# A hybrid decoder layer: feed-forward loads begun at the scores' end, token transposes further back, the bias table in other banks

## The chip, the cores and the metric

The kernel runs on one core of a Trainium2 chip. The metric is the device time of one execution in microseconds, lower is better. A core has a matrix engine (PE, its weight loads shown as PEld), a vector engine (DVE), an activation engine (ACT), a general engine (POOL) and a queue engine (SP). SP and POOL start the DMA transfers between HBM and on-chip memory; POOL can also start one that adds what it brings to what is there. Matrix products land in eight PSUM banks, which DVE and ACT read.

## The reference

One layer on a sequence of 512 tokens of 1024 values, float32. Three groups of attention heads share one input projection; their outputs are joined, projected by `w_out` (1024 x 1024) and added to `x`; a feed-forward of width 4096 and a last norm follow.

```python
h = rmsnorm(x, norm1_w)
proj = h @ w_in
aq, ak, av, bq, bk, bv, br, ba, cq, ck, cv = jnp.split(proj, ...)
y_a = dilated_attention(heads(aq, 6), heads(ak, 6), heads(av, 6), bias_a)
y_b = gla(heads(bq, 4), heads(bk, 4), heads(bv, 4), br, ba, w_a2, b_a, gla_norm_w)
y_c = moba_attention(heads(cq, 6), heads(ck, 6), heads(cv, 6), bias_c)
mix = jnp.concatenate([y_a, y_b, y_c], axis=-1)
x = x + mix @ w_out
h2 = rmsnorm(x, norm2_w)
x = x + jnp.square(jax.nn.relu(h2 @ w_ff1)) @ w_ff2
return rmsnorm(x, final_norm_w)
```

## The kernel before

**Arithmetic.** Each float32 operand of a large product is split into a high part, rounded to PE's fast format (ACT writes it, tiles `wh`, `xh`, `mh`, `yp`, `Ah`), and the rest (DVE subtracts, `wl`, `xl`, `ml`, `Al`); three products of halves (high by high, low by high, high by low) make up one. The large products are also cut into 2 x 2 blocks and done with seven block products instead of eight (`PRODUCTS`, numbered 0 to 6; the out-projection takes them in `O_ORDER` = 0, 1, 3, 5, 2, 4, 6). The weights of products 2 to 6 are sums of quarters of the matrix, formed either by loads on POOL that accumulate in the raw buffer `wraw` or by DVE. Every weight goes the same way: SP loads 512 KB into `wraw`, ACT and DVE split it (`parts`), PE uses it. `ip` 0 and 1 are the two halves of a product's inner dimension.

**Stages in time.** Projections and gated attention, to about 100 us (`qkps` are PE's products of queries and keys for the projections, `vt` the bias table); scores, softmax and values (`sps`, `ptp`, `po`), to about 200; the out-projection (`ops`), about 185 to 245, whose results DVE adds to `x` (tiles `x3`, shown as `x`); the root mean square of each token (`m`, `tmp`, `y`), the scaled tokens (`y0`, shown as `y`), their transposes on PE into a bank `yps`, and the copies out of it (`yf`), from which the feed-forward's token parts `yp` are made; then the feed-forward until 561: `f1X`, `f1Y` and `f1Z` are its first layer, `f2X` and so on its second.

**What sets the order.** The program is written as streams: generators that yield one instruction or a group of matmuls at a time. A planner (`Plan`) runs them once, before anything is built, keeps a clock for each engine from a cost for every instruction, and always issues the instruction that could begin first, with a stream's priority as the second key (lower first). A stream can `take` and `give` a resource (a PSUM bank of the pools "mm", "s", "pt", "o" and "g", a weight slot "w", a buffer "big", a raw slot "rawo"), `wait` for a key that another stream fires, or `spawn` a stream. What comes out is a fixed order on each engine; a change of one wait moves rows far from it, on every engine.

**The streams that the change touches.** `bias_table` makes the table of relative biases in two products on PE; `fetch_o` loads the out-projection's weights and `cut_o` splits them; `out_proj` issues its matmuls; `y_out` scales and transposes the tokens; `fetch_ff` loads the feed-forward's weights, `cut_ff` splits them, and `fewer` and `give("w")` pass weight slots between the two. The key "scores" is fired when the last scores are done, "turns" when the last attention output is turned, "o cut" when all of `w_out` is split. All instructions are recorded by one helper, so each carries line L129 in the profile; they are told apart by their tiles.

Of the kernel before, what the change touches and what calls it, by code (L numbers as in the profile page):

```python
# [100 lines left out]
class Plan:  # L101
# [14 lines left out]
    def spawn(self, gen, prio=0):  # L116
        self.streams.append(dict(gen=gen, prio=prio, item=None, at=self.now, sent=None, n=len(self.streams)))

    def fire(self, key, t=None):
        self.done[key] = self.now if t is None else t  # L120

    def give(self, res):
        self.free[res].append(self.now)
# [26 lines left out]
    def run(self):  # L150
        while self.streams:
            cand, moved = None, False
            for st in list(self.streams):
                while True:
                    if st["item"] is None:
                        try:
                            moved = True
                            self.now = st["sent"] if st["sent"] is not None else st["at"]
                            st["item"] = st["gen"].send(st["sent"])
                        except StopIteration:  # L160
                            self.streams.remove(st)
                            break
                    it = st["item"]
                    if isinstance(it, tuple):
                        kind, key = it
                        if kind == "prio":
                            st["prio"] = key
                        elif kind == "wait":
                            if key not in self.done:
                                break  # L170
                            st["at"] = max(st["at"], self.done[key])
                        else:
                            if not self.free[key]:
                                break
                            t = min(self.free[key])
                            self.free[key].remove(t)
                            st["at"] = max(st["at"], t)
                        st["sent"], st["item"] = st["at"], None
                        continue
                    o = self.best(st)  # L180
                    first = o[0] if isinstance(o, list) else o
                    t = max(self.start(x, st["at"]) for x in (o if isinstance(o, list) else [o]))
                    if cand is None or (t, st["prio"], st["n"]) < cand[:3]:
                        cand = (t, st["prio"], st["n"], st, o)
                    break
            if cand is None:
                if moved:
                    continue
                if self.streams:
                    raise RuntimeError("streams wait for ever")  # L190
                return
            t, _, _, st, o = cand
            end = 0.0
            for x in o if isinstance(o, list) else [o]:
                end = max(end, self.issue(x, t))
            st["item"], st["sent"] = None, end
# [3 lines left out]
def hybrid_block_kernel(ctx: ExitStack, tc: tile.TileContext, xT_d, x_d, w0_d, wv_d, wqk_d, wo_d, w1_d, w2_d,  # L200
# [10 lines left out]
    spawn, fire, give = plan.spawn, plan.fire, plan.give  # L211
    late = dict(copy=LC, tt=LT)

    def slot(name, dt=F32, shape=(128, 512)):
        return sp.tile(list(shape), dt, name=name, tag="slot", bufs=SLOTS)

    def big(name, dt=F32, shape=(128, 1024)):
        return wp.tile(list(shape), dt, name=name, tag="big", bufs=BIGS)
# [4 lines left out]
    def bank(tag, name):  # L223
        return ps.tile([128, 512], F32, name=name, tag=tag, bufs=BANKS[tag])
# [183 lines left out]
    def o_plus(n, ip, t, qs):  # L408
        for q in qs:
            yield POOL.dma_start(t, wo_d[q[0], q[1], ip], accum_op=OP.add)  # L410
        VB["o", n, ip] = t
        fire(("oB", n, ip))
# [8 lines left out]
                fire(("x3", t, half))  # L421

    def fetch_o():
        for n, q, more in ((0, (0, 0), None), (1, (1, 0), None), (5, (1, 1), None), (4, (0, 1), ((1, 1),)),
                           (6, (1, 0), ((0, 0), (0, 1), (1, 1)))):
            for ip in range(2):
                yield ("take", "rawo")
                yield ("take", "big")
                VB["o", n, ip] = t = big("wraw")
                yield SP.dma_start(t, wo_d[q[0], q[1], ip])  # L430
                if more:
                    spawn(o_plus(n, ip, t, more), 3)
                else:
                    fire(("oB", n, ip))

    def cut_o():
        for n in O_ORDER:
            for ip in range(2):
                yield ("wait", ("oB", n, ip))
                t = VB["o", n, ip]  # L440
                yield from parts(("o", n, ip), t)
                if n in (0, 3):
                    spawn(o_plus(2 if n else 3, ip, t, ((1 if n else 0, 1),)), 3)
                else:
                    give("rawo")
                    give("big")

        fire("o cut")

    XS = {}  # L450
    units = [(i, c) for c in range(NC) for i in (1, 2)]
# [22 lines left out]
    def give_raw():  # L474
        give("big")
        give("raw2")
# [81 lines left out]
            yield ("take", "w")  # L558

    def cut_ff():  # L560
        yield ("wait", "o cut")
        for u in units:
            for o, (n, *_) in enumerate(PRODUCTS):
                if u == units[0] or u == units[1]:
                    yield ("prio", 0.5 if u == units[0] else 3)
                if u == units[-1]:
                    if o == 0:
                        for _ in range(3):
                            give("w")
                    yield ("prio", 1.5 + o)  # L570
                for ip in range(2):
                    yield ("wait", ("B", u, n, ip))
                    yield from parts((u, n, ip), B[u, n, ip])
                    fire(("cut", u, n, ip))
                    if n in (1, 4, 6):
                        give_raw()
# [69 lines left out]
    def bias_table(oneh):  # L646
        yield ("wait", "R")
        for i in range(2):
            yield ("take", "mm")
            vt = bank("mm", "vt")  # L650
            yield PE.matmul(vt[:, :320], rb, oneh[i], start=True, stop=True)
            vals = slot("vals", shape=(12, 320))
            yield DVE.tensor_copy(vals, vt[:12, :320])
            give("mm")
            yield POOL.dma_start(tab[:, i * 320:(i + 1) * 320], vals)
        fire("tab")

# [2 lines left out]
    st = {}  # L660
# [577 lines left out]
    def y_out(t, half, y):  # L1238
        y0 = slot("y0")
        yield Any(DVE.tensor_scalar(y0, x3[t, half], y, None, op0=OP.mult), ACT.activation(y0, x3[t, half], AF.Copy, scale=y))  # L1240
        r = "og"[half] if t % 2 else "pt"
        yield ("take", r)
        pt = bank(r, "yps")
        yield [PE.transpose(pt[:, i * 128:(i + 1) * 128], y0[:, i * 128:(i + 1) * 128], ident) for i in range(4)]
        ts = slice(t % 2 * 128, t % 2 * 128 + 128)
        ks = range(half * 4, half * 4 + 4)
        src = [pt[:, i * 128:(i + 1) * 128] for i in range(4)]
        if t % 2 == 0:
            yf[half, t // 2] = [new("yf") for _ in range(2)]
        else:  # L1250
            yield ("wait", ("yf", t - 1, half))
        for i, k in enumerate(ks):
            out, scale = yf[half, t // 2][i // 2][:, i % 2, ts], nw2[:, k:k + 1]
            yield Any(ACT.activation(out, src[i], AF.Copy, scale=scale), DVE.tensor_scalar(out, src[i], scale, None, op0=OP.mult))
        give(r)
        fire(("yf", t, half))
# [50 lines left out]
    def out_proj():  # L1307
# [39 lines left out]
        for n in O_ORDER:  # L1347
            if n == 1:
                yield ("wait", "scores")
                for q in range(2):  # L1350
                    yield from part(n, q, (0, 1, 2))
                yield ("wait", "turns")
                for q in range(2):
                    yield from part(3, q, (0, 1, 2))
                spawn(fetch_ff(), 4)
                spawn(cut_ff(), 3)
                spawn(y_parts(), 0.4)
            for q in range(2):
                yield from part(n, q, (3,) if n in (1, 3) else (0, 1, 2, 3))
            give_w()  # L1360
            give_w()
            if n in (2, 3):
                give("big")
                give("big")
            if n == 2:
                give("w")
                give("w")
            give("raw2")

    hq = {}  # L1370
# [343 lines left out]
```

## Time and profile before

| | |
|---|---|
| median of three runs | 574.91 us (573.92 to 576.64) |
| profiled execution | 574.53 us, of which the span 572.8 |
| granted clock of PE over the span | 0.996 |
| PE busy | 555.9 us, 97% of the span, 3513 matmuls |
| DVE busy | 480.9 us, 84%, 879 instructions |
| ACT busy | 372.4 us, 65% |
| POOL busy | 71.1 us, 12% |
| moved by DMA | 99.73 MB, mean 174 GB/s |

The profile shows one execution. Its page gives the busy time of each engine, the chain of work that ended last, groups of instructions (output and inputs by tile name, count, mean duration, idle time before them and what ended it), and the DMA issues with the time to their landing. Beside it stand answers on the trace: waits by name, busy time by stretch, and timelines, each row with its start and duration, the instruction, and in brackets how long the engine had stood idle and what released it.

### The profile page before, as it was taken

What the parts mean: (1) busy time and instruction counts of PE and PEld (TensorE: products, weight loads), DVE (VectorE), ACT (ScalarE), POOL (GpSimd) and SP (SyncE); (2) the same over time, 40 slices, a digit from 0 to 9 for tenths busy, and PEclk for the clock granted to TensorE, in tenths of its full rate; (3) what the DMA queues carried; (4) which work ended last, traced back from release to release, by engine and by line L of the source; (5) the groups of instructions that cost most, each with busy time, mean ns of one, the idle gap of its engine ahead of it and who ended that gap; (6) DMA issues with size and microseconds to landing.
All of it is one profiled execution on the core that took longest, in us unless ns stands there. A gap on an engine that the chain in (4) does not pass through costs nothing.

```text
span 572.8 us, 9467 instructions
## 1 busy us (share of the span) xinstructions
PE 555.9 (97%) x3513; PEld 478.6 (84%) x3513; DVE 480.9 (84%) x879; ACT 372.4 (65%) x662; POOL 71.1 (12%) x93
## 2 busy tenths in 40 slices
PE   9999999999999999998999999999999999999994
PEld 8977887886786767788988899988999888999883
DVE  5899899977876988799799996799967799867993
ACT  6755644795865775788785466855467655579543
POOL 4012110001011011101212002020020110112101
PEclk9999999999999999999999999999999999999998
DMA  8944694396087549965988529787278594395812
GB/s 287 405 116 114 112 239 107 111 376 124 5 165 195 153 119 271 243 213 129 229 241 166 171 95 243 239 147 217 92 160 278 133 195 157 96 215 112 147 54 94
DMA packets 30813, 99.73 MB, mean 174 GB/s; under 512 B 3744, under 2 KB 3786, under 8 KB 30768
## 3 DMA queue, kind: packets, MB, share of 16 engines
q0 software_dynamic: 10032, 35.62, 34.4%
q1 hardware_dynamic: 20448, 63.25, 31.7%
q8 instruction: 27, 0.44, 0.3%
q10 hardware_dynamic: 288, 0.27, 0.1%
q14 instruction: 18, 0.15, 0.1%
HBM read 97.00 MB, written 2.13 MB: 173 GB/s over the span
## 4 chain that ended last, share of the span: by engine, by line
PE 85%; DVE 8%; ACT 3%; issue 1%; DMA 1%; SPq 0%; DVEq 0%; ACTq 0%
PE f2X L129 15%; PE f1X L129 15%; PE qkps L129 11%; PE f2Z L129 8%; PE f1Z L129 7%; PE vps L129 6%; PE ops L129 4%; PE f2Y L129 4%; PE f1Y L129 3%; PE sps L129 2%; PE po L129 2%; PE ptp L129 2%; DVE wl L129 2%; PE av L129 1%; DVE yf L129 1%; PE lp L129 1%
## 5 line engine op out<-in xcount | busy, mean ns | idle before, releaser
L129 DVE TENSOR_TENSOR wl<-wraw,wh 128x1024 fp32r<-128x1024 f32 (+2 forms) x174 | 191.3, 1109 | 36.0 <-ACT wh L129 35.8
L129 ACT ACTIVATE wh<-wraw 128x1024 fp32r<-128x1024 f32 (+2 forms) x173 | 164.3, 965 | 54.7 <-DVE x L129 9.7
L129 PE MATMUL f1X<-yp,wh 128*128 128x256 f32 x512 | 92.7, 283 | 0.0
L129 PEld LDWEIGHTS f1X<-yp,wh 128*128 128x128 f32 x512 | 80.1, 192 | 0.3
L129 POOL DMA_DIRECT2D wraw<-in_w x46 | 40.4, 952 | 273.8 <-DVE wl L129 205.2
L129 PE MATMUL f1X<-yp,wl 128*128 128x256 f32 x256 | 72.4, 283 | 0.0
L129 PE MATMUL f2X<-wh,Al 128*128 128x512 f32 (+1 forms) x132 | 50.5, 383 | 0.0
L129 PE MATMUL f2X<-wh,Ah 128*128 128x512 f32 (+1 forms) x132 | 50.5, 383 | 0.0
L129 PE MATMUL f2X<-wl,Ah 128*128 128x512 f32 (+1 forms) x132 | 50.5, 383 | 0.0
L129 PEld LDWEIGHTS f1X<-yp,wl 128*128 128x128 f32 x256 | 49.1, 192 | 0.0
L129 PE MATMUL f1Z<-yp,wh 128*128 128x256 f32 x256 | 46.3, 283 | 0.0
L129 PE MATMUL qkps<-xh,wh 128*128 128x512 f32 x96 | 40.8, 425 | 1.6 <-DVE vals L129 1.2
L129 ACT ACTIVATE h<-h 128x512 f32<-128x512 f32 x56 | 34.7, 625 | 11.5 <-DVE h L129 11.0
L129 PEld LDWEIGHTS f1Z<-yp,wh 128*128 128x128 f32 x256 | 39.9, 192 | 0.0
L129 ACT ACTIVATE Ah<-h 128x512 fp32r<-128x512 f32 x40 | 24.2, 620 | 22.2 <-DVE h L129 22.2
L129 PE MATMUL f1Z<-yp,wl 128*128 128x256 f32 x128 | 36.4, 284 | 1.8 <-DVE wl L129 1.8
L129 PE MATMUL qkps<-xh,wl 128*128 128x512 f32 x96 | 37.6, 392 | 0.0
L129 PE MATMUL qkps<-xl,wh 128*128 128x512 f32 x96 | 37.5, 391 | 0.0
L129 ACT ACTIVATE P<-P,mn 128x512 f32<-128x512 f32 (+3 forms) x48 | 26.5, 554 | 14.3 <-DVE mn L129 14.1
L129 PEld LDWEIGHTS f2X<-wl,Ah 128*128 128x128 f32 x132 | 24.8, 188 | 4.8
L129 PEld LDWEIGHTS f2X<-wh,Al 128*128 128x128 f32 x132 | 24.8, 188 | 4.8
L129 PEld LDWEIGHTS f2X<-wh,Ah 128*128 128x128 f32 x132 | 24.8, 188 | 4.7
(261 smaller groups left out, 1229.9 us busy)
## 6 DMA issues: line engine op xcount, KB each, us to landing
wraw<-in_w SPq DMA_DIRECT2D x66, 512.0 KB, 5.7
wraw<-in_w POOLq DMA_DIRECT2D x46, 512.0 KB, 6.4
wraw<-in_wqk SPq DMA_DIRECT2D x12, 512.0 KB, 6.5
wraw<-in_wo POOLq DMA_DIRECT2D x12, 512.0 KB, 7.4
wraw<-in_wv SPq DMA_DIRECT2D x10, 512.0 KB, 7.1
wraw<-in_wo SPq DMA_DIRECT2D x10, 512.0 KB, 6.2
wraw<-in_wv POOLq DMA_DIRECT2D x8, 512.0 KB, 5.8
nb<-tab SPq DMA_DIRECT2D x12, 256.0 KB, 4.8
```

Of the source, the lines that this page charges most:

```text
L129: getattr(getattr(self.nc, op.eng), op.method)(*op.args, **op.kw)
```

## The change

- The bias table's two products take a bank of the pool "s" (the scores' banks) instead of "mm".
- A new item of a stream, `("delay", t)`, puts its next instruction `t` us later on the planner's clock. It costs nothing on the chip. `y_out` yields 2.0 of it before the transposes.
- `fetch_ff` and `cut_ff` are spawned when the scores end, before product 1's first matmuls, instead of after product 3's first ones. `cut_ff` waits for product 4's split before it begins and for product 6's before the third of its products, instead of for all of `w_out`. The priority of product 6's split is 0.4. Two weight slots are given back after "turns" instead of after product 2.
- The weights of the out-projection's product 6 (the sum of all four quarters) are no longer loaded into their own buffer by a load on SP and three accumulating ones on POOL for each half. They are made from product 2's buffer (a sum of three quarters) by one accumulating load, after product 2 is split. On SP the loads of `w_out` go from 10 to 8, on POOL from 12 to 8.

```diff
--- before.py
+++ after.py
@@ -165,6 +165,8 @@
                         kind, key = it
                         if kind == "prio":
                             st["prio"] = key
+                        elif kind == "delay":
+                            st["at"] += key
                         elif kind == "wait":
                             if key not in self.done:
                                 break
@@ -421,8 +423,7 @@
                 fire(("x3", t, half))
 
     def fetch_o():
-        for n, q, more in ((0, (0, 0), None), (1, (1, 0), None), (5, (1, 1), None), (4, (0, 1), ((1, 1),)),
-                           (6, (1, 0), ((0, 0), (0, 1), (1, 1)))):
+        for n, q, more in ((0, (0, 0), None), (1, (1, 0), None), (5, (1, 1), None), (4, (0, 1), ((1, 1),))):
             for ip in range(2):
                 yield ("take", "rawo")
                 yield ("take", "big")
@@ -435,17 +436,19 @@
 
     def cut_o():
         for n in O_ORDER:
+            if n == 6:
+                yield ("prio", 0.4)
             for ip in range(2):
                 yield ("wait", ("oB", n, ip))
                 t = VB["o", n, ip]
                 yield from parts(("o", n, ip), t)
-                if n in (0, 3):
-                    spawn(o_plus(2 if n else 3, ip, t, ((1 if n else 0, 1),)), 3)
+                if n in (0, 3, 2):
+                    m, q = {0: (3, (0, 1)), 3: (2, (1, 1)), 2: (6, (1, 0))}[n]
+                    spawn(o_plus(m, ip, t, (q,)), 3)
                 else:
                     give("rawo")
                     give("big")
-
-        fire("o cut")
+            fire(("o cut", n))
 
     XS = {}
     units = [(i, c) for c in range(NC) for i in (1, 2)]
@@ -558,9 +561,10 @@
             yield ("take", "w")
 
     def cut_ff():
-        yield ("wait", "o cut")
         for u in units:
             for o, (n, *_) in enumerate(PRODUCTS):
+                if u == units[0] and o in (0, 2):
+                    yield ("wait", ("o cut", 6 if o else 4))
                 if u == units[0] or u == units[1]:
                     yield ("prio", 0.5 if u == units[0] else 3)
                 if u == units[-1]:
@@ -646,12 +650,12 @@
     def bias_table(oneh):
         yield ("wait", "R")
         for i in range(2):
-            yield ("take", "mm")
-            vt = bank("mm", "vt")
+            yield ("take", "s")
+            vt = bank("s", "vt")
             yield PE.matmul(vt[:, :320], rb, oneh[i], start=True, stop=True)
             vals = slot("vals", shape=(12, 320))
             yield DVE.tensor_copy(vals, vt[:12, :320])
-            give("mm")
+            give("s")
             yield POOL.dma_start(tab[:, i * 320:(i + 1) * 320], vals)
         fire("tab")
 
@@ -1238,6 +1242,7 @@
     def y_out(t, half, y):
         y0 = slot("y0")
         yield Any(DVE.tensor_scalar(y0, x3[t, half], y, None, op0=OP.mult), ACT.activation(y0, x3[t, half], AF.Copy, scale=y))
+        yield ("delay", 2.0)
         r = "og"[half] if t % 2 else "pt"
         yield ("take", r)
         pt = bank(r, "yps")
@@ -1347,13 +1352,15 @@
         for n in O_ORDER:
             if n == 1:
                 yield ("wait", "scores")
+                spawn(fetch_ff(), 4)
+                spawn(cut_ff(), 3)
                 for q in range(2):
                     yield from part(n, q, (0, 1, 2))
                 yield ("wait", "turns")
+                give("w")
+                give("w")
                 for q in range(2):
                     yield from part(3, q, (0, 1, 2))
-                spawn(fetch_ff(), 4)
-                spawn(cut_ff(), 3)
                 spawn(y_parts(), 0.4)
             for q in range(2):
                 yield from part(n, q, (3,) if n in (1, 3) else (0, 1, 2, 3))
@@ -1362,9 +1369,6 @@
             if n in (2, 3):
                 give("big")
                 give("big")
-            if n == 2:
-                give("w")
-                give("w")
             give("raw2")
 
     hq = {}
```

How rows move. First DVE, in the projections: `vals` is the copy of the bias table's bank, `tk`, `k2` and `la` belong to the stage around it. Before:

```order
L129 TENSOR_SCALAR la_561<-zps_549,bav_75 128x512
L129 TENSOR_TENSOR kB_567<-bk_122,R_96 128x512
L129 SCALAR_TENSOR_TENSOR qB_572<-bq_121,R_96 128x512
L129 COPY vals_564<-vt_557 12x320
L129 TENSOR_TENSOR tk_579<-qkps_523,R_96 128x512
L129 TENSOR_TENSOR la_561<-la_561,ab_560 128x512
L129 TENSOR_TENSOR wl_578<-wraw_421,wh_577 128x1024
L129 TENSOR_TENSOR k2_586<-tk_579,k2_586 128x512
```

and now:

```order
L129 TENSOR_SCALAR la_558<-zps_549,bav_75 128x512
L129 TENSOR_TENSOR kB_567<-bk_122,R_96 128x512
L129 SCALAR_TENSOR_TENSOR qB_572<-bq_121,R_96 128x512
L129 TENSOR_TENSOR tk_580<-qkps_510,R_96 128x512
L129 TENSOR_TENSOR la_558<-la_558,ab_557 128x512
L129 TENSOR_TENSOR wl_579<-wraw_421,wh_578 128x1024
L129 TENSOR_TENSOR k2_588<-tk_580,k2_588 128x512
L129 SCALAR_TENSOR_TENSOR b_593<-smask_81,la_558 128x512
L129 COPY vals_564<-vt_560 12x320
```

The second copy of `vals` goes from the place ahead of `tk` to five rows further back.

Second DVE, at the out-projection's end: `wl` with 128x1024 is a split of `w_out`, with 128x512 a half-split of a feed-forward weight; `x3` rows subtract or add a product, `yf` rows copy transposed tokens. Before:

```order
L129 TENSOR_TENSOR x3_2146<-x3_2146,ops_2655 128x512
L129 TENSOR_TENSOR wl_2759<-wraw_2120,wh_2758 128x1024
L129 TENSOR_TENSOR x3_2142<-x3_2142,ops_2354 128x512
L129 SCALAR_TENSOR_TENSOR m_2689<-ssq_2785,m_2689 128x1
L129 SCALAR_TENSOR_TENSOR tmp_2794<-y_2793,m_2689 128x1
L129 SCALAR_TENSOR_TENSOR y_2793<-tmp_2794,y_2793 128x1
L129 TENSOR_SCALAR y0_2804<-x3_2132,y_2793 128x512
L129 TENSOR_TENSOR x3_2146<-x3_2146,ops_2492 128x512
L129 TENSOR_SCALAR yf_2821<-yps_2807,nw2_72 128x128 x2
L129 TENSOR_SCALAR yf_2822<-yps_2807,nw2_72 128x128
L129 TENSOR_SCALAR yf_2828<-yps_2809,nw2_72 128x128
L129 TENSOR_SCALAR yf_2829<-yps_2809,nw2_72 128x128
```

and now:

```order
L129 TENSOR_TENSOR x3_2156<-x3_2156,ops_2655 128x512
L129 TENSOR_TENSOR wl_2754<-wraw_2535,wh_2753 128x512 x2
L129 TENSOR_TENSOR x3_2152<-x3_2152,ops_2386 128x512
L129 TENSOR_TENSOR wl_2775<-wraw_2537,wh_2774 128x512 x2
L129 SCALAR_TENSOR_TENSOR m_2683<-ssq_2784,m_2683 128x1
L129 TENSOR_TENSOR wl_2752<-wraw_1619,wh_2751 128x1024
L129 SCALAR_TENSOR_TENSOR tmp_2799<-y_2798,m_2683 128x1
L129 TENSOR_TENSOR x3_2156<-x3_2156,ops_2461 128x512
L129 SCALAR_TENSOR_TENSOR y_2798<-tmp_2799,y_2798 128x1
L129 TENSOR_TENSOR wl_2806<-wraw_2539,wh_2805 128x512
L129 TENSOR_SCALAR y0_2831<-x3_2142,y_2798 128x512
L129 TENSOR_SCALAR y0_2832<-x3_2152,y_2798 128x512
```

Half-splits of the feed-forward's first weights now stand ahead of product 6's first split (`wl_2752`) and of the scaled tokens `y0`; before, product 6's first split (`wl_2759`) came right after product 4's, and the first of the feed-forward's rows 24 rows later.

Third PE, at the last of four sets of token transposes (`yps`). Before:

```order
L129 MATMUL f1X<-yp,wl 128x256
L129 MATMUL yps<-cst,y_3040 128x128 x4
L129 MATMUL yps<-cst,y_3041 128x128 x4
L129 MATMUL f1X<-yp,wh 128x256 x2
L129 MATMUL f1X<-yp,wl 128x256
```

and now:

```order
L129 MATMUL f1Y<-yp,wl 128x256
L129 MATMUL yps<-cst,y_3065 128x128 x4
L129 MATMUL yps<-cst,y_3066 128x128 x4
L129 MATMUL f1Y<-yp,wh 128x256 x2
L129 MATMUL f1Y<-yp,wl 128x256
```

The set has moved from between the `f1X` matmuls to between the `f1Y` ones. In whole: before, 75 `ops` matmuls, the first set of 8 transposes, 12 `ops`, the second set, 33 `ops`, 18 `f1X`, the third, 18 `f1X`, the fourth; now 93 `ops`, the first, 12 `ops`, the second, 18 `ops`, 42 `f1X`, the third, 6 `f1X` and 6 `f1Y`, the fourth.

## The prediction

> **What bounds the kernel now.** I read the profile page first, then PE's waits, then PE's busy time by stretches, and last the timelines where PE stops. On the page:
>
> ```profile
> span 572.8 us, 9467 instructions
> PE 555.9 (97%) x3513; PEld 478.6 (84%) x3513; DVE 480.9 (84%) x879; ACT 372.4 (65%) x662; POOL 71.1 (12%) x93
> PE 85%; DVE 8%; ACT 3%; issue 1%; DMA 1%; SPq 0%; DVEq 0%; ACTq 0%
> ```
>
> PE works 555.9 of 572.8 us, so no new order can win more than 16.9 us, and the change leaves PE's matmuls as they are. The question is which of those idle microseconds it touches. The waits by name (engine, what waited, on what; total, times, longest):
>
> ```profile
> PE yps L129 <- DVE y L129: 2.2, 3, 1.2
> PE f1Z L129 <- DVE wl L129: 1.8, 2, 1.4
> PE qkps L129 <- DVE vals L129: 1.2, 1, 1.2
> PE ops L129 <- DVE x L129: 1.0, 1, 1.0
> PE qkps L129 <- DVE tq L129: 0.3, 1, 0.3
> PE ops L129 <- DVE mn L129: 0.3, 1, 0.3
> ```
>
> They sum to 6.8 us, all released by DVE. Where they lie, in stretches of the span (length, then busy time of PE, PEld, DVE, ACT and POOL with instruction counts, the granted clock, DMA share, GB/s):
>
> ```profile
> 30.00:40.00 10.00, 9.44 (x40) 6.78 (x39) 10.00 (x23) 5.17 (x9) 0.91 (x1) 1.00 0.49 115
> 40.00:50.00 10.00, 8.78 (x36) 6.50 (x36) 9.09 (x15) 4.59 (x6) 3.93 (x7) 1.00 0.48 110
> 90.00:100.00 10.00, 9.84 (x70) 7.44 (x69) 10.00 (x21) 2.87 (x3) 0.00 (x0) 1.00 0.30 69
> 210.00:220.00 10.00, 9.03 (x46) 5.97 (x44) 7.12 (x14) 5.24 (x12) 0.42 (x1) 1.00 0.99 254
> 220.00:230.00 10.00, 10.00 (x44) 8.30 (x45) 8.35 (x11) 4.42 (x6) 2.62 (x3) 1.00 0.95 268
> 230.00:240.00 10.00, 8.80 (x47) 7.15 (x47) 7.34 (x23) 6.67 (x17) 0.88 (x1) 1.00 1.03 270
> 240.00:250.00 10.00, 9.57 (x60) 8.48 (x60) 9.55 (x25) 8.90 (x24) 0.88 (x1) 1.00 0.98 242
> 250.00:260.00 10.00, 9.46 (x80) 9.26 (x79) 9.56 (x21) 7.36 (x16) 0.88 (x1) 1.00 0.49 127
> 260.00:270.00 10.00, 8.25 (x67) 7.84 (x65) 9.77 (x18) 8.79 (x18) 0.88 (x1) 1.00 0.62 148
> 270.00:560.00 290.00, 289.92 (x1834) 264.39 (x1835) 248.12 (x309) 185.35 (x263) 37.12 (x42) 1.00 0.68 169
> ```
>
> Two things are to be seen. From 230 to 270 us, where the out-projection hands over to the feed-forward, PE loses 1.20+0.43+0.54+1.75 = 3.92 us while DVE is 95 to 98% busy in the last three stretches. In the two before, 210 to 230, DVE idles 4.5 us, and 2.7 more in 230 to 240. And from 270 to 560 PE is busy for 289.92 of 290 us: whatever PE is ahead by at 270 it keeps to the end, since no wait there could swallow it.
>
> **The change, part by part.**
>
> *Bias table in the scores' banks.* Before, the table's second product takes one of the two "mm" banks, and the next projection block must wait until DVE has copied it:
>
> ```profile
> 45.95 0.47 DVE L129 COPY vals<-vt 12x320 f32<-12x320 f32 x1
> 46.48 0.50 PE L129 MATMUL qkps<-xh,wh 128*128 128x512 f32 x1 [1.22 <-DVE vals L129]
> ```
>
> With "s" banks, which are empty until the scores begin, that wait of 1.22 us has no cause left; the one of 0.3 on tq, in the same bank rotation, most likely goes with it. DVE now makes the copy later, after tk. What the copy delays is only the bias table's rows, which are loaded for the scores far behind. But DVE is 10.00 of 10 busy at 90 to 100 us and PE loses 0.16 there: PE arriving 1.5 us earlier at a DVE that is full may wait for part of it. Bounds: 0 (all given back there) and 1.5. From 100 us on PE has slack again, and the other stretch in which DVE is full, 30 to 40, lies before the wait. I take 1.3.
>
> *The 0.3 us on mn.* In the new DVE order mn no longer stands behind a subtraction of the out-projection. Bounds 0 and 0.3; I take 0.3. The 1.0 us on x at 220 is a chain between product 1's sum and product 5's first matmul on the same bank, untouched by the change: 0.
>
> *Feed-forward loads and splits sooner.* SP held its feed-forward loads until 202.69 us; the first two rows are work that the first three loads wait for in the new order:
>
> ```profile
> 190.41 0.39 PE L129 MATMUL qkps<-xh,wl 128*128 128x512 f32 x1
> 194.19 1.22 DVE L129 TENSOR_TENSOR wl<-wraw,wh 128x1024 fp32r<-128x1024 f32 x1
> 202.69 28.56 SPq L129 DMA_DIRECT2D wraw<-in_w  x10
> 241.50 0.68 DVE L129 TENSOR_TENSOR wl<-wraw,wh 128x512 fp32r<-128x512 f32 x1
> ```
>
> Now they are spawned when the scores end, and the first three wait for the last query and key products and for a split of an earlier weight, which end near 191 and 195 us. The first split (241.50 before, the 39 us between being the wait for the whole "o cut") stands in DVE's new order right behind product 4's, so at about 226. That is 15 us sooner: four half-splits of 0.60 (two take 1.28 below, one 0.68) before product 6's first split and two more soon after, some 3.6 us of DVE work out of the full stretch, 240 to 270, into one that has 4.5+2.7 us idle. What hides them is that idle time; where they stand in front of something PE waits for, they cost. Product 5's splits, which hold up PE now (the last two rows; the first is a pair of half-splits),
>
> ```profile
> 247.71 1.28 DVE L129 TENSOR_TENSOR wl<-wraw,wh 128x512 fp32r<-128x512 f32 x2
> 267.68 0.38 PE L129 MATMUL f1Z<-yp,wl 128*128 128x256 f32 x1 [0.40 <-DVE wl L129]
> 270.08 0.38 PE L129 MATMUL f1Z<-yp,wl 128*128 128x256 f32 x1 [1.44 <-DVE wl L129]
> ```
>
> stand 19 and 15 rows earlier in DVE's queue, well before PE needs them: 1.84 us go.
>
> *Token transposes further back.* The transposes wait for y, the scaled x; the first three rows give the spacing of the matmuls around them:
>
> ```profile
> 244.81 0.39 PE L129 MATMUL ops<-wl,mh 128*128 128x512 f32 x1
> 245.04 0.40 PE L129 MATMUL f1X<-yp,wh 128*128 128x256 f32 x2
> 245.27 0.28 PE L129 MATMUL f1X<-yp,wl 128*128 128x256 f32 x1
> 236.63 0.63 PE L129 MATMUL yps<-cst,y 128*128 128x128 f32 x4 [1.20 <-DVE y L129]
> 247.78 0.66 PE L129 MATMUL yps<-cst,y 128*128 128x128 f32 x4 [0.43 <-DVE y L129]
> 251.56 0.66 PE L129 MATMUL yps<-cst,y 128*128 128x128 f32 x4 [0.54 <-DVE y L129]
> ```
>
> These are the second to fourth of the four sets (the first, at 231.6, waits for nothing). PE's new order puts 18 more ops matmuls ahead of the first two sets, and 42 and 54 f1 matmuls ahead of the last two instead of 18 and 36. At 0.23 us for an ops and 0.12 for an f1 matmul (spacing of starts) that is 4.1, 2.9 and 2.2 us further back, more than each wait: 2.17 us go.
>
> So 4.01 us of waits go between 230 and 270. New ones come. Walking PE's and DVE's new orders against each other with the durations above, I find three. f1X, begun about 2 us earlier, waits for the low half of the first tokens, which follows the splits and product 6's subtraction: about 0.85. The transposes pushed back into f1Y keep their bank, and the f1Y or yf work that follows it, until later: 0.3 to 0.8. The first f1Z, whose yp DVE still makes in a full stretch: about 0.3. Together 1.8, between 0 and 4.0 (DVE the bound throughout, each microsecond gained lost again). Net 2.2.
>
> *Product 6's weights.* Two loads on SP and six accumulates on POOL (512 KB each) become two accumulates, onto the sum that product 2 leaves in its buffer. The price that is nearest, in the stretch where they fall (205 to 235 us, POOL's issues of in_wo):
>
> ```profile
> q0 software_dynamic: 734, 2.68, 47.6%
> q1 hardware_dynamic: 1137, 4.13, 39.6%
> wraw<-in_wo POOLq DMA_DIRECT2D x4, 512.0 KB, 9.0
> DMA to landing us min/median/max: 7.2/9.0/14.5
> ```
>
> An accumulate takes more of the DMA engines than a plain load: 47.6% for 2.68 MB against 39.6% for 4.13. In 205 to 235 the queues hold 87% together, so 1.5 MB of loads brought forward to before 205 and 3 MB less in all ease it. The two accumulates are issued after product 2's splits, by my walk at 219.8 and 221.8 us, and DVE comes to their splits at 228.7 and 233. The first has 8.9 us less about 1 for ACT's half of the split, so 8 to land; the second 10. At the median of 9.0 the first is 1 us late; with the queue eased I take 7.5 and no cost. Ends: 7.2 (nothing) and 14.5 (6.5 us, DVE blocked in order, everything behind it late).
>
> [...] The trace's rows agree that landing lengthens where both queues are full: 9.0 here against the page's 7.4 for all twelve.
>
> ```profile
> wraw<-in_wo POOLq DMA_DIRECT2D x12, 512.0 KB, 7.4
> ```
>
> **Sum.** 1.3 + 0.3 + 2.2 = 3.8 us off the profiled execution's own 574.53 (span 572.8 and 1.73 around it): 570.7. The median of the three runs, 574.91, lies 0.4 above it, and the runs themselves 2.7 apart. A change under 0.5%, 2.9 us, can hardly be told from none.
>
> **The rivals.**
> 1. *The waits move and don't go.* For it: DVE is 95% busy from 240 to 270, so if the splits don't fit into the idle time before (it comes in pieces of under 1 us, as the row below shows one, between the steps of an inverse root) the 4.0 us come back as waits for yp and yf. Against: the work itself moves 15 us forward. Time: 574.53 - 1.6 = 572.9; with the bias table's gain given back too, 574.2.
>
> ```profile
> 229.92 0.16 DVE L129 SCALAR_TENSOR_TENSOR m<-ssq,m 128x1 f32<-128x1 f32 x1 [0.79 <-ACT junk L129]
> ```
>
> 2. *Product 6's accumulate lands late* (slower than before). It now can't start until product 2's split has read the buffer, and DVE executes in order: behind its split stand x3's subtractions, y and more splits, and behind those PE. For it: 14.5 us for one of four in this stretch. Against: fewer transfers on POOL. It costs nothing up to about 8 us from issue, cancels the whole gain at 8+3.8 = 11.8, and at 14.5 gives 570.7+6.5 = 577.2; slower by 0.5% takes more than 15.
> 3. *All of it goes* and no new wait comes: 1.5+0.3+4.0 = 5.8 us, 568.7. Against: DVE's queue is no shorter in all.
> 4. *The middle pays.* The new priorities reshuffle rows on PE from the value projection to the scores, where PE is now busy throughout. A wait there of the size of those above, 0.3 to 1.2, twice or three times: 572 to 574, worse if one sits on DVE's full stretch.
>
> **How the numbers follow.** Chances: forecast 0.51 (its own range 569.0 to 572.0), rival 1 0.24, rival 2 0.11, rival 3 0.07, rival 4 0.07. The range leaves out rival 2 and a part of 4, about 0.14 with a margin of 0.5 for what a run varies: 568.2 to 574.8. Faster by over 0.5% means below 572.0: 0.49 of the forecast and 0.07 of rival 3, 0.56. Slower by over 0.5%, above 577.8: 0.07 of rival 2 and 0.02 of rival 4, 0.09. The rest, 0.35, lies between.
>
> **What would show it.** Bias table: no wait of qkps on vals, and PE in 40 to 50 at nearly 10. Loads: SP's first feed-forward load at about 191, the first half-split of in_w on DVE before 230. Transposes: no wait of yps over 0.2. Product 6: POOL's last two in_wo issues near 220, landed in 8 us or less, and DVE not idle before that split. Handover: f1X's first matmul near 242 instead of 245.04, and PE idle 230 to 270 at about 1.8 us instead of 3.9. I am wrong if f1X starts on time and f1Z or f1Y then wait for yp as long as f1Z did for wl; or if a wait of over 1 us stands between 50 and 200, where PE has none now.

## The result and the profile after

| | median | range | ratio to before |
|---|---|---|---|
| before | 575.12 us | 573.92 to 576.64 | 1 |
| changed | 569.86 us | 569.23 to 570.41 | 0.9903 (0.9882 to 0.9925) |

5.3 us faster (4.3 to 6.8 by the interval), where 3.8 were forecast. The page of the changed kernel:

```profile
span 567.6 us, 9462 instructions
PE 556.4 (98%) x3513; PEld 479.2 (84%) x3513; DVE 479.6 (84%) x876; ACT 372.5 (66%) x665; POOL 67.6 (12%) x89
PE 89%; DVE 7%; ACT 2%; issue 1%; DVEq 0%; ACTq 0%
```

PE has the same 3513 matmuls and is busy 0.5 us longer, so the 5.2 us of span are idle time of PE that is gone: 16.9 us before, 11.2 now, less that 0.5. Its waits now (engine, what waited, on what; total, times, longest):

```profile
PE f1Y L129 <- DVE yf L129: 1.2, 1, 1.2
PE f1X L129 <- DVE x L129: 0.8, 1, 0.8
PE ops L129 <- DVE x L129: 0.2, 1, 0.2
PE yps L129 <- DVE y L129: 0.2, 1, 0.2
PE f1X L129 <- DVE yp L129: 0.2, 1, 0.2
```

The waits on vals, tq, mn and wl are gone, yps on y has shrunk from 2.2 to 0.2, and f1Y and f1X have new ones. Stretches as before, without 220 to 230, where PE is busy throughout in both:

```profile
30.00:40.00 10.00, 10.00 (x45) 7.69 (x44) 10.00 (x23) 5.30 (x9) 0.91 (x1) 1.00 0.45 113
40.00:50.00 10.00, 9.86 (x41) 7.45 (x41) 9.68 (x16) 4.60 (x6) 3.40 (x6) 1.00 0.46 106
90.00:100.00 10.00, 9.83 (x70) 7.51 (x69) 10.00 (x23) 1.00 (x2) 0.00 (x0) 1.00 0.31 105
210.00:220.00 10.00, 9.77 (x43) 7.19 (x40) 7.66 (x16) 6.57 (x12) 0.87 (x1) 1.00 0.54 155
230.00:240.00 10.00, 9.84 (x52) 8.09 (x51) 8.42 (x23) 7.13 (x20) 0.87 (x1) 1.00 0.83 214
240.00:250.00 10.00, 8.69 (x63) 7.70 (x62) 9.54 (x24) 8.63 (x23) 2.65 (x3) 1.00 0.94 280
250.00:260.00 10.00, 9.21 (x77) 9.21 (x78) 8.72 (x20) 6.24 (x14) 0.00 (x0) 1.00 0.77 200
260.00:270.00 10.00, 10.00 (x83) 9.80 (x82) 9.77 (x17) 10.00 (x20) 3.55 (x4) 1.00 0.52 116
270.00:560.00 290.00, 290.00 (x1832) 264.20 (x1830) 245.46 (x307) 182.61 (x259) 34.58 (x38) 1.00 0.66 165
```

PE's idle time by stretch, before and now: 30 to 50 us 1.78 and 0.14; 210 to 220 0.97 and 0.23; 230 to 270 3.92 and 2.26; and 0.27 at 203, gone. That is 4.3 us. Of the rest, 0.35 lies in the first 30 us, where equal orders also differ: `qkps` begins between 29.0 and 30.3 us in the profiles of this study. Another 1.0 lies behind PE's last matmul, which begins at 564.21 and 559.97 us, 4.24 apart: the slowest transfer of the output took 3.7 us to land before and 2.7 now. That is not the change's doing as far as the traces show: from the end of PE's last matmul to the end of the span twelve of the 14 profiles take 7.3 to 7.7 us, and two, of the kernel before and of one with only product 6's part, take 8.3 and 8.4. DVE worked 7.34 of 10 us at 230 to 240 before and 8.42 now: the early splits fill its idle time there.

### The profile page after: what moved, and what is told of

Same layout as the page of the kernel before. It is cut to its first block, busy times and chain, and to the rows that moved or that the text cites. A ratio compares the mean times of both kernels' runs of the same rounds, so it can differ in the third digit from the quotient of the medians.

```text
span 567.6 us, 9462 instructions
## 1 busy us (share of the span) xinstructions
PE 556.4 (98%) x3513; PEld 479.2 (84%) x3513; DVE 479.6 (84%) x876; ACT 372.5 (66%) x665; POOL 67.6 (12%) x89
## 3 DMA queue, kind: packets, MB, share of 16 engines
q0 software_dynamic: 9456, 33.53, 32.8%
## 4 chain that ended last, share of the span: by engine, by line
PE 89%; DVE 7%; ACT 2%; issue 1%; DVEq 0%; ACTq 0%
PE f2X L129 15%; PE f1X L129 15%; PE qkps L129 10%; PE f1Z L129 8%; PE f2Z L129 8%; PE vps L129 6%; PE f1Y L129 4%; PE f2Y L129 4%; PE ops L129 4%; PE sps L129 3%; PE ptp L129 2%; PE po L129 2%; PE av L129 2%; DVE wl L129 2%; PE lp L129 1%
## 5 line engine op out<-in xcount | busy, mean ns | idle before, releaser
L129 DVE TENSOR_TENSOR Al<-h,Ah 128x512 fp32r<-128x512 f32 x40 | 26.7, 684 | 3.4 <-ACT Ah L129 3.4
```

The costliest lines, as they stand in the source:

```text
L129: getattr(getattr(self.nc, op.eng), op.method)(*op.args, **op.kw)
```

## Experiments

Two sets of four undo one part each and do one part alone; four more test what these showed. Each set was timed beside the kernel before, and ratios are to that.

### One part taken out of the changed kernel

Bias table back in "mm":

```diff
-            yield ("take", "s")
-            vt = bank("s", "vt")
+            yield ("take", "mm")
+            vt = bank("mm", "vt")
```

> The changed kernel with the bias table back in the "mm" banks; PE's order from the scores to the end is the changed kernel's. Theory (each part is worth the waits at its place): the wait of qkps on vals returns, 1.2 to 1.6 us, and nothing makes it up later: about 571.4 us against 569.9, ratio to before 0.993. Rival (PE's earlier arrival is given back where DVE is full, 90 to 100 us): within 0.3 us of the changed kernel, 569.9.

572.12 us, 0.9939 (0.9923 to 0.9955): 1.8 us of the gain gone, by 0.9907 for the changed kernel run again, below. PE's 30 to 50 us in this kernel and in the changed one:

```profile
30.00:50.00 20.00, 18.25 (x76) 13.21 (x75) 19.05 (x37) 10.15 (x16) 4.85 (x8) 1.00 0.47 115
```

```profile
30.00:50.00 20.00, 19.86 (x85) 15.14 (x84) 19.68 (x38) 9.90 (x15) 4.31 (x7) 1.00 0.46 110
```

1.61 us of PE's time are back as waits (vals 1.2, tq 0.3), and 90 to 100 gives nothing back. The theory holds; 1.8 in the medians and its 1.2 to 1.6 can't be told apart.

Without the delay:

```diff
-        yield ("delay", 2.0)
```

> The changed kernel without the 2 us of delay: PE has its token transposes 3 to 24 matmuls sooner. Theory: the waits of yps on y return in part, 0.5 to 1.5 us, and the wait of f1Y on yf (1.2 us in the changed kernel) goes in part: about 570.5 us. Rival 1 (the delay only trades one wait for another): 569.9. Rival 2 (the transposes' waits of 2.2 us were what the change took away): 572.

568.52 us, 0.9882 (0.9866 to 0.9897): faster than the changed kernel, which no theory had. Its second and fourth sets of transposes wait for y:

```profile
234.82 0.41 PE L129 MATMUL yps<-cst,y 128*128 128x128 f32 x2 [0.56 <-DVE y L129]
248.95 0.33 PE L129 MATMUL yps<-cst,y 128*128 128x128 f32 x1 [1.24 <-DVE y L129]
```

1.80 us, and 0.13 on ACT's y beside, where the changed kernel idles 2.26 in the handover. So the delay trades waits, at a loss. Where the changed kernel loses them, PE and then DVE:

```profile
242.32 0.36 PE L129 MATMUL f1X<-yp,wh 128*128 128x256 f32 x1 [0.76 <-DVE x L129]
250.79 0.39 PE L129 MATMUL f1Y<-yp,wh 128*128 128x256 f32 x1 [1.19 <-DVE yf L129]
239.85 1.13 DVE L129 TENSOR_SCALAR yf<-yps,nw 128x128 f32<-128x128 f32 x4 [0.44 <-ACT yf L129]
240.90 0.68 DVE L129 TENSOR_TENSOR wl<-wraw,wh 128x512 fp32r<-128x512 f32 x1
241.50 0.68 DVE L129 TENSOR_TENSOR x<-x,ops 128x512 f32<-128x512 f32 x1
```

f1X takes the bank that DVE empties with x at 241.50, and that x stands behind the copies yf of the transposes and a split. Later transposes mean later copies, in front of work that PE needs. f1Y takes the bank of the third set, which the last copies empty.

Feed-forward begun as before (the spawns after product 3's first matmuls, `("wait", "o cut")` ahead of all splits, the two slots given back after product 2, and no priority of 0.4 for product 6's split):

```diff
-                spawn(fetch_ff(), 4)
-                spawn(cut_ff(), 3)
                 for q in range(2):
                     yield from part(n, q, (0, 1, 2))
...
+                spawn(fetch_ff(), 4)
+                spawn(cut_ff(), 3)
```

> The changed kernel with feed-forward loads and splits begun as before (after product 3's first matmuls, splits only after all of w_out). Theory: the first split of in_w is back at about 240 us on DVE, the waits of f1Z on wl return (1.8 us) with some of yps: 571.9 to 572.5 us. Rival (the delay and the shorter chain of product 6 suffice): 570 to 570.4, no f1Z wait over 0.3.

573.24 us, 0.9967 (0.9954 to 0.9979): 3.4 us of the gain gone, more than the theory's 2 to 2.6. Its waits on weights are these (`m` is the row that follows product 6's second split on DVE, which ends at 240.34 where the wait ends at 240.39):

```profile
PE f1X L129 <- DVE wl L129: 1.0, 2, 0.7
PE ops L129 <- DVE m L129: 0.9, 1, 0.9
PE f1Z L129 <- DVE wl L129: 0.9, 1, 0.9
```

And yps waits 2.3 on y, the delay notwithstanding.

Product 6's weights loaded as before:

```diff
-        for n, q, more in (..., (4, (0, 1), ((1, 1),))):
+        for n, q, more in (..., (4, (0, 1), ((1, 1),)),
+                           (6, (1, 0), ((0, 0), (0, 1), (1, 1)))):
...
-                if n in (0, 3, 2):
+                if n in (0, 3):
```

> The changed kernel with product 6's weights loaded as before, 2 loads on SP and 6 accumulates on POOL, 3 MB more. Theory: the feed-forward's loads begin as early and DVE's order is nearly the same, so it costs only what the fuller queues delay, 0 to 1.0 us: 570.3. Rival 1 (product 6's accumulates in POOL's queue hold up the feed-forward's own): 572, with waits of f1X or f1Z on wl or on a DMA. Rival 2 (they cost nothing; product 2's chain was the later one): 569.6.

575.07 us, 1.0007 (0.9995 to 1.0018): without this part nothing is left of the gain. All three theories were far off. PE, at the scores' end, and DVE:

```profile
200.88 0.83 PE L129 MATMUL sps<-k,q 64*128 64x256 f32 x6 [1.47 <-DVE mn L129]
202.13 0.50 PE L129 MATMUL ops<-wh,mh 128*128 128x512 f32 x1 [0.42 <-DVE mn L129]
...
204.07 0.63 PE L129 MATMUL ops<-wh,ml 128*128 128x512 f32 x1
204.50 0.63 PE L129 MATMUL ops<-wl,mh 128*128 128x512 f32 x1
```

```profile
199.45 0.69 DVE L129 TENSOR_TENSOR x<-x,ops 128x512 f32<-128x512 f32 x1 [0.32 <-PE ops L129]
200.06 0.55 DVE L129 CUSTOM_DVE_ANT_0 P<-sps,nb 128x384 f32<-128x384 f32 x1
200.53 0.08 DVE L129 DVE_READ_ACCUMULATOR2_ANT mn<- 128x1 f32 x1
```

An x subtraction of the out-projection stands in DVE's queue ahead of the scores' minimum mn. It waits for PE's last ops matmul, and PE, whose next rows need mn, then waits for mn: 1.9 us. Behind that the ops matmuls start 0.43 us apart, not 0.23: the granted clock falls to half (0.50 from 203 to 205 us). Stretches of the kernel without this part, and of the changed one:

```profile
200.00:202.00 2.00, 0.83 (x6) 0.60 (x6) 1.79 (x12) 1.36 (x6) 0.00 (x0) 1.00 1.00 215
202.00:206.00 4.00, 3.87 (x11) 3.04 (x12) 4.00 (x18) 2.55 (x9) 0.00 (x0) 0.57 1.05 266
```

```profile
200.00:202.00 2.00, 2.00 (x14) 1.57 (x11) 1.71 (x8) 2.00 (x9) 0.00 (x0) 1.00 0.74 252
202.00:206.00 4.00, 4.00 (x27) 3.40 (x26) 3.20 (x11) 3.55 (x10) 0.00 (x0) 1.00 0.02 7
```

0.57 over 4 us is 1.7 us of clock lost. With the 1.9 of waits that is 3.6 of the 5.7 us. Three short waits of ops at 220 to 223 add 0.7 against the changed kernel, and the handover 0.6 (2.9 against 2.3, the longest f1Z's 1.35 on yp). All 12 executions of this kernel have a granted clock of 0.994 or less, all ten of the changed one 0.995 or more.

### Is it the order or the transfers?

The kernel just told keeps its order and loses four of the six accumulates on the chip, so that two quarters are missing from product 6's weights:

```diff
+            op.left_out = n == 6 and q != (1, 1)
...
-        getattr(getattr(self.nc, op.eng), op.method)(*op.args, **op.kw)
+        if not getattr(op, "left_out", False):
+            getattr(getattr(self.nc, op.eng), op.method)(*op.args, **op.kw)
```

> The kernel without product 6's change (loads on SP, accumulates on POOL, 575.1 us), in its exact order on PE, DVE and ACT, but four of product 6's six accumulates are left out on the chip (two quarters of its weights are missing from its sums), so 2 MB less is moved. Theory (the 5 us came from the order that the planner made of it, a subtraction of x that stands ahead of the last scores' minimum on DVE, and from the lower clock after that stall): no gain, 574.5 to 575.1 us, the wait of sps on mn still 1.5 us and the granted clock 0.5 behind it. Rival (the transfers themselves, POOL's queue and the late loads): 570 to 571.5 us.

575.02 us, 1.0001 (0.9990 to 1.0011), to 0.1 us the time with them. 33.53 MB by POOL's queue instead of 35.62 bring nothing, so what was lost lies in the order and not in these transfers (the two remaining accumulates and the loads on SP stayed). The waits of 1.47 and 0.42 us stand there unchanged, and so does the half clock (0.57 from 202 to 206 us). In the profiled execution it has lost the clock a second time besides. This is its 262 to 268 us and, under it, those of the kernel with all transfers, in the same place of the same order, both behind a wait of f1Z of 1.36 and 1.35 us:

```profile
262.00:268.00 6.00, 5.73 (x35) 5.73 (x36) 6.00 (x11) 4.77 (x10) 0.00 (x0) 0.72 0.01 3
```

```profile
262.00:268.00 6.00, 5.72 (x47) 5.72 (x48) 6.00 (x11) 4.83 (x10) 0.00 (x0) 1.00 0.02 4
```

### How much delay?

The changed kernel again, beside two with less delay:

> The changed kernel once more, beside the kernels of this call. 569.9 us, ratio 0.990 to before.

569.39 us, 0.9907 (0.9888 to 0.9927).

```diff
-        yield ("delay", 2.0)
+        if t == 3:
+            yield ("delay", 1.5)
```

> The changed kernel with the delay kept only for the last of the four sets of transposes (1.5 us); the first three stand as without any delay, the fourth 6 f1X matmuls (0.7 us) further back. Theory (the delay pays only where y is late: without any, the fourth set waits 1.24 us on y and the second 0.56; with it everywhere, f1X and f1Y wait 2.1 for x and yf): 0.5 to 0.7 us better than without delay, 567.9 us, ratio to before 0.987 to 0.988. Rival (what the fourth set doesn't wait, f1Y waits): as without delay, 568.5, or as the changed kernel, 569.9.

567.71 us, 0.9877 (0.9856 to 0.9899), as the theory had it. The fourth set waits 0.52 instead of 1.24, and f1Y doesn't wait.

```diff
-        yield ("delay", 2.0)
+        yield ("delay", 1.0)
```

> The changed kernel with 1.0 us of delay instead of 2.0: the second, third and fourth sets of transposes stand 3 ops, 9 and 6 f1X matmuls further back than without delay. Theory: between the two, 568.3 to 569.3 us, with some of the second and fourth sets' waits on y gone and some of f1X's on x there. Rival (a set pushed back never costs anything, only 2.0 is too much): 567.5, no waits over 0.3 in the handover.

567.37 us, 0.9870 (0.9852 to 0.9889): the fastest kernel of the study, below the theory's 568.3 and near the rival's 567.5, though waits of yps remain:

```profile
245.66 0.33 PE L129 MATMUL yps<-cst,y 128*128 128x128 f32 x1 [0.89 <-DVE y L129]
249.15 0.33 PE L129 MATMUL yps<-cst,y 128*128 128x128 f32 x1 [0.25 <-DVE y L129]
```

From 230 to 270 PE idles 1.14 us in it, 1.23 in the one before, 1.93 without delay and 2.26 in the changed kernel. Between the first two the times can't tell; against the changed kernel beside them the runs don't overlap (567.01 to 568.22 against 568.56 to 571.79). Without delay, timed in another set, the ratios 0.9882 and 0.9907 have intervals that overlap.

### One part alone

Each is the part of the diff, on the kernel before.

> The kernel before with the bias table in the "s" banks and nothing else. Theory (worth the waits at its place, 1.57 us, which the kernel without this part showed): 573.1 us, ratio 0.997. Rival (the handover's new order, in which the last set of transposes is split in two, takes it back): 574.5.

576.36 us, 1.0020 (1.0006 to 1.0033): slower, by little more than the noise. PE is 1.3 us ahead when `lp` begins (56.32 against 57.58), so the part does its work at its place. But with its clock shifted the planner comes to the same bad order at the scores' end, with the wait

```profile
201.82 0.38 PE L129 MATMUL sps<-k,q 64*128 64x256 f32 x1 [1.47 <-DVE mn L129]
```

where the kernel before has 0.27. At 200 to 210 us PE idles 2.01 us instead of 0.27, which takes back what 30 to 50 had won. The rest of the 1.2 us isn't in this profile: its execution is the fastest of the twelve, 575.06. The others go up to 578.29 and the granted clock down to 0.990; that the stall costs them clock, as above, is likely and not shown.

> The kernel before with product 6's weights made from product 2's buffer and nothing else. PE's order differs from row 773 on, at the last scores. Theory (its worth is the order that the planner makes of it there: the waits of ops on mn and of 0.7 us on x go): 573.7 us, with the handover's waits as before. Rival 1 (3 MB less to move speeds the loads up, the feed-forward's weights come sooner): 572 or less. Rival 2 (alone it is worth nothing, since only together with early loads was there a bad order to be undone): 574.7.

576.36 us, 1.0018 (1.0005 to 1.0031). The waits on mn and of 0.7 on x go, as the theory said, but it is slower, not faster: product 6's own matmuls now wait.

```profile
241.16 0.50 PE L129 MATMUL ops<-wh,mh 128*128 128x512 f32 x1 [0.44 <-ACT wh L129]
242.68 0.50 PE L129 MATMUL ops<-wl,mh 128*128 128x512 f32 x1 [0.78 <-DVE m L129]
```

The accumulates were issued at 220.9 and 222.8, 2.2 us behind the changed kernel, as all of its out-projection is (`ops` begins at 194.48 against 192.31), and landed by 230.6. But ACT begins to split them at 235.01 and 240.06, DVE at 236.99 and 241.40, and DVE's second split, with `m` behind it, ends the second wait. So the weights were there, and the splits stand late in the queues; in the changed kernel DVE has them at 228.27 and 232.27. The priority of 0.4 for product 6 belongs to the feed-forward's part and is missing here. That it is the reason is likely, but it was not tried by itself.

> The kernel before with the feed-forward's loads and splits begun sooner and nothing else. Theory: the waits of f1Z on wl (1.8 us) go, those of yps on y stay, and the scores' end keeps the order with product 6's old loads, so a wait there of 0.3 to 1.9 us as without product 6's part: 573 to 575 us. Rival (the early splits pay in full alone): 572.5.

573.08 us, 0.9963 (0.9951 to 0.9975): 2.1 us faster alone, near the theory's lower end. It is the only part that pays by itself.

> The kernel before with the delay of 2.0 us alone. Theory (the planner's delay trades waits of yps on y for others, 2.0 is more than it needs, and it cost 1.0 us beside the other parts): 574.5 to 575.5 us. Rival (it takes the three waits of yps away, 2.2 us): 572.5.

574.88 us, 0.9995 (0.9983 to 1.0006): nothing, as the theory had it. The waits of yps on y fall from 2.2 us, and those of f1X on wl come to 1.9.

Alone the four come to +1.2 + 1.2 - 2.1 - 0.3 = 0.0 us; together to -5.3. Taken out one at a time they come to 1.8 + 3.4 + 5.7 - 1.4 = 9.5. So the parts don't add up: what one is worth hangs on the order that the others leave, as the stalls at the scores' end show.

## Why the prediction came out right

**Bias table: right, slightly small.** 1.3 taken of 1.5; 1.6 measured at its place, 1.8 in the medians. The give-back at 90 to 100 (0.16 idle before, 0.17 now) didn't happen. What the step had wrong is that the part stands by itself: alone it wins nothing, since an order 150 us further on takes the gain back.

**The 0.3 on mn: right. The 1.0 on x "untouched: 0": wrong.** It fell to 0.23. The chain is the same and as long: from the end of the last `po` to the end of the x subtraction that releases the matmul it takes 6.6 us in both. But PE now has 27 ops matmuls to do in that time where it had 24; three at 0.23 us are the 0.7 us. The forecast looked at the chain and not at what the new order puts beside it.

**Feed-forward sooner: right, and the largest sure part.** SP's first load was issued at 189.88 us (about 191 forecast), the first half-split ran at 223.87 (226), f1X began at 242.32 (242), and f1Z's 1.84 us of waits are gone:

```profile
189.88 1.29 SPq L129 DMA_DIRECT2D wraw<-in_w  x3
223.87 1.28 DVE L129 TENSOR_TENSOR wl<-wraw,wh 128x512 fp32r<-128x512 f32 x2
```

The part is worth 3.4 us when taken out and 2.1 alone. Without it yps waits on y as long as before (2.3 us), so it made room for y's chain too.

**Transposes: the wrong step.** The 2.17 us were booked as the delay's. Without any delay 0.37 of them are gone already, and the delay's own waits cost more than the 1.6 it removes. The count behind them was off as well: 15 more ops matmuls stand ahead of the first two sets, not 18, since the new order has three fewer ahead of the last `po`; 3.4 us instead of 4.1, still more than the waits. The three new waits were foreseen as f1X 0.85, f1Y 0.3 to 0.8, f1Z 0.3, together 1.8. They are f1X 0.91 (x 0.76 and yp 0.15), f1Y 1.19, f1Z none, together 2.10, and 0.16 of yps stays: net 1.75 where 2.2 was forecast. The sum came near since both its sides were seen; what was missed is that the second side was the price of one part, which was better left smaller.

**Product 6: right as far as it went, and far too small.** Issued at 218.7 and 220.6 (219.8 and 221.8 forecast); from issue to landing (least, median and most of POOL's two issues of in_wo at 217 to 222 us) they took

```profile
DMA to landing us min/median/max: 5.5/5.8/6.1
```

where 7.5 was taken; the first split then waits for ACT's half (0.47 us), not for the transfer, and DVE reaches it at 228.27 (228.7 forecast). So rival 2 did not come. The median of 9.0 us that such an accumulate took in the kernel before, at 205 to 235 us, did not come back: the two landed in 5.5 to 6.1 us though the DMA share was 1.00 from 220 to 230. And the fuller queues cost nothing: with 2 MB less in the same order the time was the same to 0.1 us. But the step priced the part by its transfers alone. Its worth lies in the order that the planner makes of it: 5.7 us when it is taken out. The forecast had no term for that.

**The sum.** 1.6 + 0.3 + 0.7 + 1.75 = 4.35 us of waits at named places, 0.35 in the first 30 us, against 1.3 + 0.3 + 0 + 2.2 forecast. The lead at 270 us is kept: PE is busy for 290.00 of 290 behind it, as argued. The number is near for the right places, though the cause of the handover's part was given to the wrong edit, and the 0.7 on x made up for 0.45 too much in the handover.

Two more things bear on the step from these 4.35 to the measured 5.3, and the forecast had neither. One is the 1.0 us of the last transfers, which the two profiles show; how it is in the other executions is not recorded. The other is the clock, of which 3.4 us at half, as in the profile of the kernel without product 6's part, are 0.003 of the span: the forecast went from a profiled execution at 0.996, but of 68 executions of the kernel before 22 have 0.994 or less, with a median of 575.9 us against 574.75 for the other 46. None of the changed kernel's ten is as low. By these numbers it is an estimated 0.4 us of the gain on average. So that the sum fell short by no more than 1.5 is partly luck.

## What to carry to other kernels

Where a planner sets the order, price an edit by the waits in the order it yields, not by the work it removes: here a part that moves 3 MB less was worth 5.7 us, and leaving out 2 of the 3 in an unchanged order was worth nothing; three of four parts were worth nothing or less alone. Pushing back what waits is no gain if its results then stand in front of other work in an engine's order (here f1X then waited 0.76 us for x and f1Y 1.19 for yf); vary the size of the push (0, 1 and 2 us gave 568.5, 567.4 and 569.4) before keeping it. And take each part out of the whole as well as trying it alone, since for the bias table and product 6 the two answers differed in sign.

## What was not expected of the hardware

With 1.9 us of waits PE lost another 1.7 us in clock. In the kernel without product 6's part the waits of 1.47 and 0.42 us came close together, and the granted clock went to 0.50 for 3.4 us.

Not every such stall did this. Rows from three profiles (length, busy time of PE, PEld, DVE, ACT and POOL, granted clock, DMA share, GB/s), each time 3.41 us around the wait, as long as the clock was at 0.50 in the first of them, and the 3.41 us behind; first the kernel without product 6's part:

```profile
199.15:202.56 3.41, 1.53 (x10) 0.98 (x9) 2.90 (x15) 2.65 (x9) 0.00 (x0) 1.00 1.00 202
202.56:205.97 3.41, 3.41 (x11) 2.63 (x10) 3.41 (x13) 2.10 (x9) 0.00 (x0) 0.50 1.05 267
```

Around f1Z's wait of 1.35 us the same kernel keeps its clock of 1.00, and with 1.36 the one with four accumulates less goes to 0.50:

```profile
260.59:264.00 3.41, 2.06 (x15) 1.86 (x16) 3.41 (x7) 1.76 (x3) 0.00 (x0) 1.00 0.31 62
264.00:267.41 3.41, 3.41 (x30) 3.41 (x30) 3.41 (x7) 3.32 (x7) 0.00 (x0) 1.00 0.00 0
```

```profile
260.30:263.71 3.41, 1.82 (x13) 1.62 (x14) 3.41 (x7) 2.04 (x4) 0.00 (x0) 1.00 0.34 67
263.71:267.12 3.41, 3.41 (x19) 3.41 (x18) 3.41 (x7) 2.98 (x6) 0.00 (x0) 0.50 0.02 5
```

The kernel before keeps it too, with waits on wl of 0.40 us, just ahead of these rows, and of 1.44, within them:

```profile
267.76:271.17 3.41, 1.97 (x15) 1.77 (x16) 3.41 (x7) 2.89 (x7) 0.00 (x0) 1.00 0.02 6
271.17:274.58 3.41, 3.41 (x31) 3.41 (x30) 3.41 (x7) 3.29 (x7) 0.87 (x1) 1.00 0.78 253
```

So the length of the longest wait does not tell: with 1.35 and 1.44 us the clock stayed, with 1.36 it fell. Of the 14 profiles only two show it below 1.00 between 10 and 560 us, that of the kernel without product 6's part and that of the one with four accumulates less. What decides is not shown here, and neither is a profile of the kernel before in one of its executions at a lower clock.
